# Two-operand elementwise work moved from GpSimd to VectorE in a one-core hybrid decoder step

## The chip, the cores and the metric

The kernel runs on one core of one Trainium2 chip. The metric is device time in microseconds of one execution. Five engines run their own instruction streams in order: TensorE (PE, with its weight loads as PEld), VectorE (DVE), ScalarE (ACT), GpSimd (POOL) and SyncE (SP), which issues most of the DMAs.

## The reference

One inference step of one decoder layer is computed in float32 for a prompt of 2048 tokens and for 8 sequences of 8 new tokens. With `D_MODEL = 1024`:

```
h = rmsnorm(x, norm_attn);  p = h @ w_in                      # 1024 -> 4608 columns
o_attn = sliding-window attention with sinks(p[q, k, v])
o_rwkv = rwkv7_mixer(p[rwkv part])                            # token shift, decay, matrix state, group norm
gates  = sigmoid(p[gate part] + b_gate)
merged = gates[:1024] * (o_attn @ w_branch_attn) + gates[1024:] * (o_rwkv @ w_branch_rwkv)
x = x + merged @ w_out
u = rmsnorm(x, norm_ffn) @ w_ffn_in
x = x + (gelu(causal_conv3(u[:D_FF])) * u[D_FF:]) @ w_ffn_out # D_FF = 2816
y = rmsnorm(x, norm_final)
```

The outputs are y and the new caches and states.

## The kernel before, in words

**Tiling.** The 2112 tokens are three blocks of 704, each cut in halves of 384 and 320 columns. Activations lie with features on the partitions. A weight matrix is cut in units of 128 x 1024 (512 KB): 108 for `w_in`, 24 each for the branches and for `w_out`, 132 and 66 for the two FFN matrices, over the three blocks. Each float32 value is split in a high part, rounded to the matmul type, and a low part, the difference; `mm3` (L366) multiplies high by high, high by low and low by high, so each 128-row step of a half takes three matmuls.

**A unit of weights.** `unit` loads a unit with an SP DMA, writes its high part on ACT (L347) and its low part (L353) on DVE or POOL: the counter `nw` sends every third unit to DVE, in one instruction of 1024 columns, the other two to POOL, in two instructions of 512 columns each. There are two buffers, so a unit is split while the one before it is being multiplied.

**Other two-operand work on POOL.** Part of the sums of squares for the norms (`square`, L407); the low parts of the attention queries, of half the normed inputs and of the inputs of the head sums (`split`, L358, through `halves`, `normed` and `parts`); keys times their factors in `prep` (L921, L926); the sum of the two gated branches in `branches` (L1367); and every second row of the last output (L1531 in `final_last`). POOL also does fills (memset) and two casts at the start.

**Stages.** `run` computes the inputs of the three blocks, then per block the branches, the merge and the FFN. Beside these main matmuls, which write the PSUM tiles `psd`, runs background work in generators: attention, the 64-token chunks of the RWKV recurrence, the block inverses (62 small DVE steps and two DVE transposes per half, L1088 to L1096), the `prep` of the RWKV operands, and norms.

**Order of the work.** Before each step of `mm3`, `tick` asks a planner whether a background step may go in. `account` adds the modelled cost of each instruction (`cost`) to a clock per engine, and `open` holds a step back while DVE's or ACT's clock is over 2.0 us, or POOL's over 4.0 us, ahead of PE's. `drain` runs what is left of a stream where its result is needed. Each engine runs its stream in the order in which the scheduler of the framework, which works with its own simulated times, has put it. In `account` a POOL two-operand instruction sets a window, and a DVE instruction without a PSUM operand that would start in it is put off to its end:

```
if engine == "Pool" and type(ins).__name__ == "InstTensorTensor":
    self.locked = start, start + c
elif engine == "DVE" and self.locked[0] <= start < self.locked[1] and not any(
        hasattr(a, "bass_ap") and a.bass_ap.tensor.name.startswith("ps") for a in ins.ins):
    start = self.locked[1] - 0.2
t[engine] = start + c
```

Of the kernel before, what the change touches and what calls it, by code (L numbers as in the profile page):

```python
# [100 lines left out]
class Kernel:  # L101
    def __init__(self, tc, i, o, es):
        self.tc, self.nc, self.i, self.o, self.es = tc, tc.nc, i, o, es
        pool = lambda name, bufs, **k: es.enter_context(self.pool(name, bufs, **k))
        self.cp = pool("cst", 1)
        self.dp = pool("dram", 1, space=bass.MemoryType.DRAM)
        self.sp = pool("small", 2)
        self.tp = pool("tmp", 3)
        self.wr = pool("wraw", 2)
        self.wp = pool("wsplit", 2)  # L110
        self.kp_ = pool("keep", 3)

        self.pb = {k: pool("ps" + k, n, space=bass.MemoryType.PSUM) for k, n in (("d", 3), ("r", 3), ("c", 2))}
        self.nw, self.ahead = 0, {}
# [5 lines left out]
        self.taken, self.locked = 0, (0.0, 0.0)  # L120

# [95 lines left out]
    @staticmethod  # L217
    def cost(ins, engine):
        n = 1
        for _, k in ins.outs[0].ap[1:]:  # L220
            n *= k
        if engine == "PE":
            if ins.ins[0].dtype == F32R:
                return 0.0135 + 0.000417 * n
            if ins.is_transpose:
                return 0.11 * n / 128
            if n <= 2:
                return 0.223
            return max(0.03, 0.01 + 0.00168 * n * math.prod(ins.tile_size) / (P * P))
        kind = type(ins).__name__  # L230
        if engine == "Activation":
            return 0.12 + 0.00084 * n
        two = kind == "InstTensorTensor"
        if engine == "Pool":
            return 0.1 + (0.0024 if two else 0.0009) * n
        if kind == "InstStreamTranspose":
            return 0.06 + 0.0019 * n
        full = [a for a in ins.ins if hasattr(a, "ap") and math.prod(k for _, k in a.ap[1:]) > 1]
        return 0.1 + (0.0012 if len(full) > 1 else 0.0009) * n
# [6 lines left out]
    def account(self):  # L246
# [4 lines left out]
        for k in range(self.seen, m):  # L251
# [18 lines left out]
            else:  # L270
                start = max(t[engine], t["PE"])
                if engine == "Pool" and type(ins).__name__ == "InstTensorTensor":
                    self.locked = start, start + c
                elif engine == "DVE" and self.locked[0] <= start < self.locked[1] and not any(
                        hasattr(a, "bass_ap") and a.bass_ap.tensor.name.startswith("ps") for a in ins.ins):
                    start = self.locked[1] - 0.2
                t[engine] = start + c
                self.chained = max(self.chained + c + 0.06, t[engine])
# [61 lines left out]
    def unit(self, src, w=None):  # L340
# [6 lines left out]
        nc.scalar.copy(w[:, 0], raw)  # L347
        eng = nc.gpsimd if self.nw % 3 else nc.vector
        self.nw += 1
        step = 1024 if eng is nc.vector else 512  # L350
        for u in range(0, 1024, step):
            sl = slice(u, u + step)
            eng.tensor_tensor(w[:, 1, sl], raw[:, sl], w[:, 0, sl].bitcast(F32), op=ALU.subtract)  # L353
        return w

    def split(self, hi, lo, src, eng=None):
        self.nc.scalar.copy(hi, src)  # L357
        (eng or self.nc.vector).tensor_tensor(lo, src, hi.bitcast(F32), op=ALU.subtract)  # L358

# [9 lines left out]
    def parts(self, pool, src, n, bufs=1):  # L369

        t = pool.tile([P, 2, 384], F32R, tag="parts", name="parts", bufs=bufs)
        self.split(t[:, 0, :n], t[:, 1, :n], src, self.nc.gpsimd)
        return t
# [21 lines left out]
    def squares(self, acc, x, k, n):  # L395

        nc = self.nc
        for u in range(2):
            self.square(acc[:, :n], x[:, u], k + u, n, nc.vector)

    def square(self, acc, x, k, n, eng):
        if k == 0:
# [3 lines left out]
        self.nc.scalar.activation(sq[:, :n], x, ACT.Square)  # L406
        eng.tensor_tensor(acc, acc, sq[:, :n], op=ALU.add)  # L407

# [30 lines left out]
    def normed(self, h, k, c0, n, x, pb):  # L439
# [3 lines left out]
        nc.vector.scalar_tensor_tensor(t[:, :n], x, self.par("norm_attn", k), pb[:, :n], op0=ALU.mult, op1=ALU.mult)  # L443
        self.split(h[:, k, 0, c0:c0 + n], h[:, k, 1, c0:c0 + n], t[:, :n], nc.gpsimd if k % 2 else nc.vector)

# [17 lines left out]
    def start(self, hp, xp):  # L463
# [23 lines left out]
        accs = []  # L487
        for x, (c0, n), eng in zip(xs, HALF, (nc.vector, nc.gpsimd)):
            acc = self.tp.tile([P, 384], F32, tag="acc", name="acc", bufs=2)
            accs.append(acc)  # L490
            for k in range(KT):
                self.scaled(self.h, k, c0, n, x[:, k, :n], "norm_attn")
                self.square(acc[:, :n], x[:, k, :n], k, n, eng)
        self.setup()
# [28 lines left out]
    def load_x(self, b, xp):  # L523
# [7 lines left out]
        for c0, n in HALF:  # L531
            acc = self.tp.tile([P, 384], F32, tag="acc", name="acc", bufs=2)
            for k in range(KT):
                self.square(acc[:, :n], self.xn[:, k, c0:c0 + n], k, n, nc.vector if k % 2 else nc.gpsimd)
                yield 1.0
# [112 lines left out]
    def attn_prompt(self, b, ap, t0=0, t1=T):  # L648
# [25 lines left out]
        def halves(f):  # L674
# [4 lines left out]
            k2 = ap.tile([P, 2, 256], F32R, tag="k2", name="k2")  # L679
            self.split(q2[:, 0, :, :, :nq], q2[:, 1, :, :, :nq], q[:, :, :, :nq], nc.gpsimd)  # L680
            nc.scalar.copy(k2[:, :, :nk], k[:, :, :nk])
# [202 lines left out]
    def prep(self, b, p, hf, xk, xv, xr, pp, st):  # L884
# [35 lines left out]
        nc.vector.tensor_scalar(kp[:, :n], at[:, :n], self.kah[:, p:p + 1], self.kah1[:, p:p + 1], op0=ALU.mult, op1=ALU.add)  # L920
        nc.gpsimd.tensor_tensor(kp[:, :n], kp[:, :n], xk, op=ALU.mult)  # L921
        kb = pp.tile([P, 6, 128], F32, tag="kb", name="kb")
        for sg in sgs:
            for r_ in range(2):
                rows = slice(r_ * 64, r_ * 64 + 64)
                nc.gpsimd.tensor_tensor(self.chv(kb, sg, rows, r_), self.pl(kp, sg)[rows], self.v65(ei, sg, 1)[rows], op=ALU.mult)  # L926

# [422 lines left out]
    def branches(self, b, os_, ms, gts, x):  # L1350

        nc = self.nc
        for j in range(8):
# [4 lines left out]
            for c0, n in HALF:  # L1358
                m = []
                for br in range(2):  # L1360
# [17 lines left out]
    def merge(self, b, x, ms, xp, op):  # L1378
# [14 lines left out]
        for j, hf in ((j, hf) for j in range(8) for hf in range(2)):  # L1393
# [7 lines left out]
            self.scaled(h2, j, c0, n, xv, "norm_ffn")  # L1401
            self.square(accs[hf][:, :n], xv, j, n, nc.vector if j == KT - 1 else nc.gpsimd)
            if j == KT - 1:
# [70 lines left out]
    def final(self, b, x):  # L1474
# [5 lines left out]
        def done(hf, j):  # L1480
            c0, n = HALF[hf]
            if j == 0:
                accs.append(self.tp.tile([P, 384], F32, tag="acc", name="acc", bufs=2))
            self.square(accs[hf][:, :n], x[:, j, c0:c0 + n], j, n, nc.gpsimd)
            if j == KT - 1:
# [29 lines left out]
    def final_last(self, b, x, fp):  # L1515
# [25 lines left out]
        def done(hf, j):  # L1541
            c0, n = HALF[hf]
            acc, xv = accs[hf][:, :n], x[:, j, c0:c0 + n]
            self.square(acc, xv, j, n, nc.gpsimd if j < 6 else nc.vector)
            if j == KT - 1:
# [254 lines left out]
```

## Time and profile before

| what | before |
|---|---|
| median of 3 runs (lowest to highest) | 3327.91 us (3327.47 to 3331.76) |
| the profiled execution: its time, and its span | 3327.79 us, 3326.0 us |
| mean granted TensorE clock | 0.988 |
| busy: PE, DVE, ACT, POOL | 98%, 59%, 36%, 30% |

The time of the profiled execution is 1.79 us longer than its span, from the first instruction to the last. A row of a group of instructions gives the line, the engine, the operation, the tiles written and read with their shape, the count, the busy time in us with the mean of one in ns, and the idle time of that engine just before them with what ended it. A row of the timeline gives start and duration in us of one instruction, or of a run of equal ones. A row of the waits says which engine and line waited for which, for how long in total, how often, and the longest.

### The profile page before, as it was taken

To read this page: it belongs to the slowest core of one execution; us is meant where nothing else is said; L and a number is where in the kernel's file an instruction comes from. 1 tells how busy PE (TensorE), PEld (TensorE's weight loads), DVE (VectorE), ACT (ScalarE), POOL (GpSimd) and SP (SyncE) were. 2 spreads that over 40 slices of the span, in tenths; PEclk is the share of its full clock that TensorE was granted. 3 is DMA by queue.
4 is the path that set the end of the run, shared out by engine and by line. 5 is a ranking of instruction groups with operands and counts; after the bars stand their busy time and mean duration, and the time that the engine had idled before them with its cause. 6 is when DMAs were issued, how large, how long until landed. Compare 5 with 4: busy or idle time off the path is not lost.

```text
span 3326.0 us, 60594 instructions
## 1 busy us (share of the span) xinstructions
PE 3250.5 (98%) x24072; PEld 3131.5 (94%) x24072; DVE 1948.6 (59%) x4058; ACT 1213.4 (36%) x2274; POOL 1010.1 (30%) x878
## 2 busy tenths in 40 slices
PE   8999998999999899999999999999999999999998
PEld 8998998999999789899999999999999999999998
DVE  7676568735563466577455558745456465444545
ACT  4455433333333567523232333332233233222223
POOL 3332433323223244132222254222122353222223
PEclk9999999999999899999999999999999999999999
DMA  4643443545653744233532363253313272122222
GB/s 136 182 141 117 140 152 118 146 130 159 200 171 119 221 144 118 73 80 105 153 118 87 111 225 96 82 168 110 112 65 130 70 257 70 64 70 70 70 65 75
DMA packets 335164, 408.96 MB, mean 123 GB/s; under 512 B 110496, under 2 KB 261152, under 8 KB 334624
## 3 DMA queue, kind: packets, MB, share of 16 engines
q1 hardware_dynamic: 330720, 399.31, 38.8%
q10 hardware_dynamic: 4160, 5.77, 0.5%
q8 instruction: 190, 3.11, 0.4%
q14 instruction: 94, 0.77, 0.1%
HBM read 307.55 MB, written 98.41 MB: 122 GB/s over the span
## 4 chain that ended last, share of the span: by engine, by line
PE 71%; DVE 3%; DMA 1%; issue 1%; ACT 0%; POOL 0%; SPq 0%; POOLq 0%; DVEq 0%; ACTq 0%
PE psd L366 62%; PE psr L694 1%; PE psr L743 1%; PE psc L1162 1%; PE psc L1195 1%; PE psc L1192 1%; DVE qt L1088 1%; DVE qb L1090 1%; PE psr L730 1%; DMA xd<-x 0%; PE psr L992 0%; PE psc L1019 0%; PE psc L1197 0%; PE psc L1291 0%; PE psc L1189 0%
## 5 line engine op out<-in xcount | busy, mean ns | idle before, releaser
L366 PE MATMUL psd<-o,wp 128*128 128x320 f32 (+1 forms) x8640 | 1453.6, 326 | 21.1 <-ACT o L357 10.8
L366 PEld LDWEIGHTS psd<-o,wp 128*128 128x128 f32 x8640 | 1400.9, 189 | 32.6 <-ACT o L357 11.8
L353 POOL TENSOR_TENSOR wp<-wr,wp 128x512 fp32r<-128x512 f32 x470 | 648.1, 1400 | 1675.7 <-ACT wp L347 1595.9
L366 PE MATMUL psd<-h,wp 128*128 128x320 f32 (+1 forms) x5184 | 918.1, 330 | 15.2 <-ACT wp L347 7.4
L366 PEld LDWEIGHTS psd<-h,wp 128*128 128x128 f32 x5184 | 838.4, 190 | 30.8 <-ACT wp L347 7.4
L347 ACT CAST wp<-wr 128x1024 fp32r<-128x1024 f32 x354 | 370.6, 1047 | 647.7 <-PE psd L366 587.6
L366 PE MATMUL psd<-ff,wp 128*128 128x384 f32 (+1 forms) x3168 | 526.7, 325 | 0.0
L366 PEld LDWEIGHTS psd<-ff,wp 128*128 128x128 f32 x3168 | 510.8, 188 | 3.1 <-DVE up L1434 0.2
L1470 DVE TENSOR_TENSOR x<-x,psd 128x384 f32<-128x384 f32 (+1 forms) x288 | 148.2, 519 | 236.9 <-PE psd L366 236.7
L1441 DVE TENSOR_TENSOR gb<-psd,rb 128x64 f32<-128x64 f32 (+2 forms) x154 | 70.5, 470 | 241.2 <-PE psd L366 223.7
L353 DVE TENSOR_TENSOR wp<-wr,wp 128x1024 fp32r<-128x1024 f32 x119 | 148.1, 1244 | 88.5 <-ACT wp L347 84.7
L1444 DVE SCALAR_TENSOR_TENSOR cc<-gb,pt,cc 128x704 f32<-128x704 f32 (+1 forms) x132 | 165.1, 1251 | 33.8 <-ACT cc L1442 33.0
L1442 ACT ACTIVATE cc<-gb,pt 128x64 f32<-128x64 f32 (+2 forms) x154 | 95.7, 636 | 188.6 <-DVE gb L1441 187.2
L407 POOL TENSOR_TENSOR acc<-acc,sq 128x320 f32<-128x320 f32 (+1 forms) x93 | 95.0, 1023 | 115.5 <-ACT sq L406 97.4
L1453 ACT ACTIVATE cc<-cc 128x704 f32<-128x704 f32 x66 | 52.4, 793 | 189.0 <-DVE cc L1444 119.1
L358 DVE TENSOR_TENSOR ff<-cc,ff 128x384 fp32r<-128x384 f32 (+1 forms) x132 | 92.9, 706 | 47.0 <-ACT ff L357 46.6
L1434 DVE TENSOR_TENSOR up<-psd,rb 128x384 f32<-128x384 f32 (+1 forms) x132 | 68.6, 520 | 51.7 <-PE psd L366 51.3
L357 ACT CAST ff<-cc 128x384 fp32r<-128x384 f32 (+1 forms) x132 | 63.9, 486 | 78.7 <-DVE cc L1456 78.1
L1090 DVE TENSOR_TENSOR qb<-qb,qt 128x31 f32<-128x31 f32 (+15 forms) x186 | 88.9, 478 | 4.1
L1088 DVE TENSOR_TENSOR qt<-nb,qb 128x31 f32<-128x31 f32 (+15 forms) x186 | 84.6, 455 | 3.2
L1367 POOL TENSOR_TENSOR m<-m 128x384 f32<-128x384 f32 (+1 forms) x48 | 48.8, 1018 | 118.4 <-DVE m L1364 85.2
L1456 DVE TENSOR_TENSOR cc<-cc,up 128x384 f32<-128x384 f32 (+1 forms) x132 | 71.2, 542 | 16.7 <-ACT cc L1453 13.5
(257 smaller groups left out, 3124.2 us busy)
## 6 DMA issues: line engine op xcount, KB each, us to landing
wr<-in_w_fi SPq DMA_DIRECT2D x132, 512.0 KB, 3.5
wr<-in_w_in SPq DMA_DIRECT2D x108, 512.0 KB, 4.0
wr<-in_w_fo SPq DMA_DIRECT2D x66, 512.0 KB, 3.5
cm<-md SPq DMA_DIRECT2D x33, 512.0 KB, 4.8
gt<-gd SPq DMA_DIRECT2D x48, 352.0 KB, 4.4
md<-m SPq DMA_DIRECT2D x48, 256.0 KB, 3.4
wr<-in_w_br SPq DMA_DIRECT2D x24, 512.0 KB, 4.7
wr<-in_w_out SPq DMA_DIRECT2D x24, 512.0 KB, 3.6
```

What stands on the lines that cost most here:

```text
L347: nc.scalar.copy(w[:, 0], raw)
L353: eng.tensor_tensor(w[:, 1, sl], raw[:, sl], w[:, 0, sl].bitcast(F32), op=ALU.subtract)
L358: (eng or self.nc.vector).tensor_tensor(lo, src, hi.bitcast(F32), op=ALU.subtract)
L366: nc.tensor.matmul(ps[:, :n], w[:, a, wk * 128:(wk + 1) * 128], act[:, k0 + k, b, c0:c0 + n], start=(start and k == 0 and j == 0), stop=(s ...
L407: eng.tensor_tensor(acc, acc, sq[:, :n], op=ALU.add)
L1088: nc.vector.tensor_tensor(tv, nb[:, s + 1:, s:s + 1].to_broadcast([P, k, s + 1]), qb[:, s:s + 1, :s + 1].to_broadcast([P, k, s + 1]), op=A ...
L1090: nc.vector.tensor_tensor(qb[:, s + 1:, :s + 1], qb[:, s + 1:, :s + 1], tv, op=ALU.add)
L1441: nc.vector.tensor_tensor(dst, view(ps, 0), view(rb, c0), op=ALU.mult)
L1442: nc.scalar.activation(view(c, c0), dst, ACT.Identity, bias=self.par("cb", f), scale=cw[2])
L1444: nc.vector.scalar_tensor_tensor(c[:, :npr], gb[:, u:u + npr], cw[u], c[:, :npr], op0=ALU.mult, op1=ALU.add)
L1456: nc.vector.tensor_tensor(cv, cv, up[:, c0:c0 + n], op=ALU.mult)
L1470: nc.vector.tensor_tensor(xv, xv, ps[:, :n], op=ALU.add)
```

## The change

All moved instructions go from POOL to DVE. A unit's low part is always one DVE instruction of 1024 columns; `split` and `square` lose the choice of engine. In the planner the cost of a POOL instruction becomes that of a fill, and the window that put DVE off goes. POOL keeps the fills, the two casts and the multiplications of L1531, which the diff doesn't touch.

```
-        two = kind == "InstTensorTensor"
         if engine == "Pool":
-            return 0.1 + (0.0024 if two else 0.0009) * n
+            return 0.1 + 0.0009 * n
...
-                start = max(t[engine], t["PE"])
-                if engine == "Pool" and type(ins).__name__ == "InstTensorTensor":
-                    self.locked = start, start + c
-                elif engine == "DVE" and self.locked[0] <= start < self.locked[1] and not any(
-                        hasattr(a, "bass_ap") and a.bass_ap.tensor.name.startswith("ps") for a in ins.ins):
-                    start = self.locked[1] - 0.2
-                t[engine] = start + c
+                t[engine] = max(t[engine], t["PE"]) + c
...
-        eng = nc.gpsimd if self.nw % 3 else nc.vector
-        self.nw += 1
-        step = 1024 if eng is nc.vector else 512
-        for u in range(0, 1024, step):
-            sl = slice(u, u + step)
-            eng.tensor_tensor(w[:, 1, sl], raw[:, sl], w[:, 0, sl].bitcast(F32), op=ALU.subtract)
+        nc.vector.tensor_tensor(w[:, 1], raw, w[:, 0].bitcast(F32), op=ALU.subtract)
...
-    def split(self, hi, lo, src, eng=None):
+    def split(self, hi, lo, src):
         self.nc.scalar.copy(hi, src)
-        (eng or self.nc.vector).tensor_tensor(lo, src, hi.bitcast(F32), op=ALU.subtract)
+        self.nc.vector.tensor_tensor(lo, src, hi.bitcast(F32), op=ALU.subtract)
...
-        eng.tensor_tensor(acc, acc, sq[:, :n], op=ALU.add)
+        self.nc.vector.tensor_tensor(acc, acc, sq[:, :n], op=ALU.add)
...
-        nc.gpsimd.tensor_tensor(kp[:, :n], kp[:, :n], xk, op=ALU.mult)
+        nc.vector.tensor_tensor(kp[:, :n], kp[:, :n], xk, op=ALU.mult)
...
-                nc.gpsimd.tensor_tensor(self.chv(kb, sg, rows, r_), self.pl(kp, sg)[rows], self.v65(ei, sg, 1)[rows], op=ALU.mult)
+                nc.vector.tensor_tensor(self.chv(kb, sg, rows, r_), self.pl(kp, sg)[rows], self.v65(ei, sg, 1)[rows], op=ALU.mult)
...
-                nc.gpsimd.tensor_tensor(m[0][:, :n], m[0][:, :n], m[1][:, :n], op=ALU.add)
+                nc.vector.tensor_tensor(m[0][:, :n], m[0][:, :n], m[1][:, :n], op=ALU.add)
```

The callers of `split` and `square` (`parts`, `halves`, `normed`, `start`, `load_x`, `merge`, `final`, `final_last`) drop their engine argument.

## Rows read from the trace of the kernel before

**Rows 1.** The page's first part: span, then busy time of each engine

```profile
span 3326.0 us, 60594 instructions
PE 3250.5 (98%) x24072; PEld 3131.5 (94%) x24072; DVE 1948.6 (59%) x4058; ACT 1213.4 (36%) x2274; POOL 1010.1 (30%) x878
```

**Rows 2.** The waits of PE: who waited for whom, total us, times, longest

```profile
PE psd L366 <- ACT o L357: 10.8, 2, 7.9
PE psr L1053 <- DVE nwyd L392: 8.2, 2, 5.5
PE psd L366 <- ACT wp L347: 7.4, 1, 7.4
PE psr L1053 <- DVE rbk L1031: 5.8, 1, 5.8
...
PE psd L366 <- DVE wp L353: 3.8, 2, 3.6
PE psd L366 <- DVE p L520: 3.8, 2, 2.1
PE psc L1053 <- DVE nwyd L392: 3.4, 1, 3.4
...
PE psr L980 <- DVE kb L961: 1.9, 3, 1.3
...
PE psd L366 <- POOL wp L353: 0.8, 1, 0.8
```

**Rows 3.** The chain that ended last: its longest piece, start, us, what

```profile
2813.07 491.58 PE psd L366 x3051
```

**Rows 4.** The timeline of PE at 295 us, with the wait ahead of it

```profile
294.88 5.49 PE L366 MATMUL psd<-h,wp 128*128 128x384 f32 x16 [2.06 <-DVE p L520]
```

**Rows 5.** Groups of instructions by line on POOL, over the whole span

```profile
L353 POOL TENSOR_TENSOR wp<-wr,wp 128x512 fp32r<-128x512 f32 x470 | 648.1, 1400 | 1675.7 <-ACT wp L347 1595.9 <-DVE S L1200 17.3 <-DVE o L358 15.3
L407 POOL TENSOR_TENSOR acc<-acc,sq 128x320 f32<-128x320 f32 (+1 forms) x93 | 95.0, 1023 | 115.5 <-ACT sq L406 97.4 <-DVE nwyr L387 5.0 <-ACT xs L837 4.3
L926 POOL TENSOR_TENSOR kb<-kp,ei 64x384 f32<-64x384 f32 (+3 forms) x56 | 50.5, 901 | 3.7
```

**Rows 6.** Groups of instructions by line on DVE, over the whole span

```profile
L353 DVE TENSOR_TENSOR wp<-wr,wp 128x1024 fp32r<-128x1024 f32 x119 | 148.1, 1244 | 88.5 <-ACT wp L347 84.7 <-POOL parts L358 1.5 <-issue 1.0
L1456 DVE TENSOR_TENSOR cc<-cc,up 128x384 f32<-128x384 f32 (+1 forms) x132 | 71.2, 542 | 16.7 <-ACT cc L1453 13.5
L961 DVE SCALAR_TENSOR_TENSOR kb<-at,ei 64x384 f32<-64x384 f32 (+3 forms) x56 | 34.0, 607 | 0.5
```

**Rows 7.** The timeline near the end, 3285 to 3290 us

```profile
3285.25 3.11 POOL L353 TENSOR_TENSOR wp<-wr,wp 128x512 fp32r<-128x512 f32 x2 [4.84 <-ACT wp L347]
3285.71 1.51 DVE L1444 SCALAR_TENSOR_TENSOR cc<-gb,pt,cc 128x640 f32<-128x640 f32 x1 [0.82 <-ACT cc L1442]
...
3288.37 0.87 DVE L1444 SCALAR_TENSOR_TENSOR cc<-gb,pt,cc 128x640 f32<-128x640 f32 x1
```

**Rows 8.** The timeline of DVE: first and last of 342 lengthened instructions

```profile
24.25 0.65 DVE L387 TENSOR_SCALAR nwyd<-rmsm 128x3 int32<-128x3 int32 x1
...
3308.01 0.70 DVE L390 SCALAR_TENSOR_TENSOR nwtd<-nwyd 128x3 f32<-128x3 f32 x1
```

**Rows 9.** The timeline of DVE, 561 to 570 us, before PE's wait for rbk

```profile
561.44 0.98 DVE L390 SCALAR_TENSOR_TENSOR nwtr<-nwyr 128x12 f32<-128x12 f32 x1
...
565.13 0.17 DVE L390 SCALAR_TENSOR_TENSOR nwtr<-nwyr 128x12 f32<-128x12 f32 x1
...
568.26 1.19 DVE L391 TENSOR_TENSOR nwtr<-nwtr,hsmr 128x12 f32<-128x12 f32 x1
```

**Rows 10.** The timeline of DVE, 2066 to 2071 us, before PE's wait for wp

```profile
2066.35 2.17 DVE L1094 STREAM_TRANSPOSE t<-qb 128x1024 f32<-128x1024 f32 x1
...
2068.41 1.87 DVE L1096 STREAM_TRANSPOSE qinv<-qb 128x1024 f32<-128x1024 f32 x1
```

**Rows 11.** Busy time per engine in one stretch: PE, PEld, DVE, ACT, POOL, clock

```profile
1996.00:2079.00 83.00, 79.42 (x486) 78.98 (x485) 73.84 (x129) 28.82 (x48) 38.87 (x36) 0.98 0.33 95
```

More of the change, by code (lines that the diff above doesn't have):

```diff
@@ L113, in __init__ @@
         self.pb = {k: pool("ps" + k, n, space=bass.MemoryType.PSUM) for k, n in (("d", 3), ("r", 3), ("c", 2))}
-        self.nw, self.ahead = 0, {}
+        self.ahead = {}
         self.streams = {}
@@ L119, in __init__ @@
         self.seen, self.chained, self.free = 0, 0.0, deque([0.0] * 3, 3)
-        self.taken, self.locked = 0, (0.0, 0.0)
+        self.taken = 0
     def pool(self, name, bufs=1, **k):
@@ L371, in parts @@
         t = pool.tile([P, 2, 384], F32R, tag="parts", name="parts", bufs=bufs)
-        self.split(t[:, 0, :n], t[:, 1, :n], src, self.nc.gpsimd)
+        self.split(t[:, 0, :n], t[:, 1, :n], src)
         return t
@@ L398, in squares, with square @@
         for u in range(2):
-            self.square(acc[:, :n], x[:, u], k + u, n, nc.vector)
-    def square(self, acc, x, k, n, eng):
+            self.square(acc[:, :n], x[:, u], k + u, n)
+    def square(self, acc, x, k, n):
         if k == 0:
@@ L443, in normed @@
         nc.vector.scalar_tensor_tensor(t[:, :n], x, self.par("norm_attn", k), pb[:, :n], op0=ALU.mult, op1=ALU.mult)
-        self.split(h[:, k, 0, c0:c0 + n], h[:, k, 1, c0:c0 + n], t[:, :n], nc.gpsimd if k % 2 else nc.vector)
+        self.split(h[:, k, 0, c0:c0 + n], h[:, k, 1, c0:c0 + n], t[:, :n])
     @staticmethod
@@ L487, in start @@
         accs = []
-        for x, (c0, n), eng in zip(xs, HALF, (nc.vector, nc.gpsimd)):
+        for x, (c0, n) in zip(xs, HALF):
             acc = self.tp.tile([P, 384], F32, tag="acc", name="acc", bufs=2)
@@ L492, in start @@
                 self.scaled(self.h, k, c0, n, x[:, k, :n], "norm_attn")
-                self.square(acc[:, :n], x[:, k, :n], k, n, eng)
+                self.square(acc[:, :n], x[:, k, :n], k, n)
         self.setup()
@@ L533, in load_x @@
             for k in range(KT):
-                self.square(acc[:, :n], self.xn[:, k, c0:c0 + n], k, n, nc.vector if k % 2 else nc.gpsimd)
+                self.square(acc[:, :n], self.xn[:, k, c0:c0 + n], k, n)
                 yield 1.0
@@ L679, in halves @@
             k2 = ap.tile([P, 2, 256], F32R, tag="k2", name="k2")
-            self.split(q2[:, 0, :, :, :nq], q2[:, 1, :, :, :nq], q[:, :, :, :nq], nc.gpsimd)
+            self.split(q2[:, 0, :, :, :nq], q2[:, 1, :, :, :nq], q[:, :, :, :nq])
             nc.scalar.copy(k2[:, :, :nk], k[:, :, :nk])
@@ L1401, in merge @@
             self.scaled(h2, j, c0, n, xv, "norm_ffn")
-            self.square(accs[hf][:, :n], xv, j, n, nc.vector if j == KT - 1 else nc.gpsimd)
+            self.square(accs[hf][:, :n], xv, j, n)
             if j == KT - 1:
@@ L1483, in done @@
                 accs.append(self.tp.tile([P, 384], F32, tag="acc", name="acc", bufs=2))
-            self.square(accs[hf][:, :n], x[:, j, c0:c0 + n], j, n, nc.gpsimd)
+            self.square(accs[hf][:, :n], x[:, j, c0:c0 + n], j, n)
             if j == KT - 1:
@@ L1543, in done @@
             acc, xv = accs[hf][:, :n], x[:, j, c0:c0 + n]
-            self.square(acc, xv, j, n, nc.gpsimd if j < 6 else nc.vector)
+            self.square(acc, xv, j, n)
             if j == KT - 1:
```

## The prediction

> **What bounds the kernel now.** I read the page's first part, then the waits of PE, then the chain and PE's timeline. PE is busy 3250.5 of 3326.0 us, DVE 59%, POOL 30% [rows 1]: TensorE's work is the bound and the change takes none of it away. What it can act on is the 75.5 us in which PE stands idle, and matmuls that run slowly for want of operands. Most of that idle time is visible in the waits of PE [rows 2], and the reader should sort it. The 7.4 us for the first weights and the 10.8 us at the first stage change, where inputs of the next stage come by DMA and are split on ACT, have no two-operand POOL work ahead of them. Four waits end on DVE work in the inputs of the blocks, where POOL works beside DVE: rbk 5.8, p 3.8, the norm's nwyd on psc 3.4, kb 1.9, together 14.9 us. The two waits on nwyd with psr, 8.2, are in the last 20 us. POOL itself ends only 0.8 us of PE's waiting, and low parts of weights on DVE end 3.8.
>
> Idle time isn't all. In the longest undisturbed piece 3051 matmuls take 491.58 us, 161 ns each [rows 3]. After one of the waits for p, 16 matmuls take 5.49 us instead of 2.6 [rows 4]: a stall goes on as slow matmuls that the page counts as busy, here 2.9 us behind a wait of 2.06. For the four waits I estimate 6 us of such tails, taking well under half of their 14.9 us because this row is one of the bad ones. So 20.9 us stand behind late DVE work.
>
> **What moves, in DVE time.** 470 POOL instructions on weights, 1.40 us each, become 235 on DVE; with 93 sums of squares and 56 key products that is 793.6 us of POOL's 1010.1 [rows 1, 5]. On DVE a unit's low part takes 1.244 us, an addition of 384 or 320 columns 0.542, a key product by its like 0.607 [rows 6]: 235 x 1.244 = 292, 93 x 0.542 = 50, 56 x 0.607 = 34, in all 377 us. The other 216.5 us of POOL are smaller moved groups and fills that stay; at the ratio of the sums of squares, 50 to 95, they are at most 115 us on DVE. I take 95, as most of them move: DVE gets about 470 us.
>
> **What DVE gets back.** With POOL at a low part, a DVE multiply-add of 640 columns takes 1.51 us; the same one, after POOL is done, 0.87 [rows 7]. Going through DVE's timeline, 342 single instructions that overlap a two-operand POOL instruction are over 0.1 us longer than the shortest tenth of their own shape, from the norm of the start, 0.65 us, to that of the end, 0.70 [rows 8]; summed, 264 us. This goes away with its cause. DVE then is busy for 1948.6 + 470 - 264 = 2155 us, 65% of the span. So a nearly doubled list of large work costs DVE only six points, and it is still not the bound. Two extra effects follow: small steps of a latency chain no longer wait behind POOL, and a unit's low part is done in 1.24 instead of 2.8 us once DVE gets to it.
>
> **What this is worth at PE.** The best-shown wait is rbk. Ahead of it seven small steps of the inverse root stretch over 8 us; the first took 0.98 and the last 1.19, while the same step between them, without POOL, took 0.17 [rows 9]. Over all seven the time beyond 0.17 is 5.5 us, almost the whole wait. But POOL's work of that stretch now stands in DVE's queue: two sums, one product, two key products, one low part of the head sum and one unit, 4 x 0.542 + 2 x 0.607 + 1.244 = 4.6 us [rows 6]. If all of it is queued ahead of rbk the gain is 0.9 us, if none, 5.5. I take the middle, 3.2 of 5.8, or 55%, since half of those instructions have no part in the norm and the queue is ordered by when each is ready. Applied to 20.9 us that is **-11.5**; the ends are 16% of 14.9, -2.4, and 95% of 20.9, -19.9. The 0.8 us behind POOL's low parts goes: **-0.8**.
>
> **What new waits cost.** Each unit's low part now stands in DVE's one queue. Behind it stand the DVE work of the main stage and the background, and PE needs it by the third matmul of the unit. Of the 119 units that were there before, PE waited for 3.8 us in all; at that rate 235 more cost 7.5 us. But 3.6 of the 3.8 are one wait, behind the two block transposes of an inverse, 2.17 + 1.87 us [rows 2, 10]; it is one event and no rate, and the queue in front of it was itself lengthened by POOL. I take half, **+3.7**, with 0 and 7.5 as ends. In the last 20 us ten sums of squares join DVE, 10 x 0.542 = 5.4 us, between additions that it makes at the pace of PE, while some of the small steps there get back 0.5 each [rows 8]; the last multiplications on POOL stay, and so does the wait behind them. I take **+0.5**, between -0.5 and +1.5. The branch sums, queries and normed inputs cost nothing: their consumers are a stage later, or the background, and the cover is PE's own work. If it went, each would add its own half microsecond at a stage change. Fewer POOL instructions touch no DMA: POOL issues none here, and SP's queue keeps its order.
>
> **Sum.** 3327.8 (this execution; 0.1 below the median of the runs) - 11.5 - 0.8 + 3.7 + 0.5 = 3319.7; I predict **3320**, against the median 0.24% less. A measurement of this kernel can tell about 0.2%, 6.7 us, from no change, so this is just beyond it. With all terms at their good ends it is 3306; the bad ends pass into the next case.
>
> **Rival 1: hidden anyway.** The moved work fills just the room that POOL's absence frees: 470 in, 264 out. If the queue is mostly ahead of the norm chains, the gain is -2.4 - 0.8, the new waits are +3.7 + 0.5, and the time is 3328.8. For it: PE is 98% busy, and 7.4 + 10.8 + 8.2 us of its idle time [rows 2] are not touched. Against it: the seven steps of rows 9, which were slow for no other reason. It holds from 3321.2 to 3334.5.
>
> **Rival 2, slower: late low parts.** An inverse ends with two transposes, 4.0 us that can't be split, and there are six inverses. Two in three units were on POOL and passed by them; now every unit's low part that comes due there stands behind them. Four more such waits of 3.6 us with the small gain and the tail's loss give 3327.8 + 14.4 - 3.2 + 0.5 = 3339.5. It decides from three or four hits on, where 3.6 each outweigh the 12.3 us of gain. For it: in the stretch of the merge and the inverse DVE is busy for 73.84 of 83 us before anything is added [rows 11]. Against it: POOL's 38.87 us there lengthen DVE's work too, and the scheduler knows the transposes. By the Trainium skill (Perfetto Trace Analysis, section Optimizing Scalar/DVE Operations) giving some work of a saturated VectorE to GpSimd may make sense, and taking it back, as here, would be a loss; the same section adds that the two share a port into SBUF, so that such a move might not help. The trace bears out the second half, by the pair in rows 7; the first half applies only in the stretch of rows 11, as DVE is at 59% on the whole.
>
> **Rival 3, slower: the planner holds background back.** DVE's clock now carries every unit with a room of 2.0 us, where POOL's had 4.0, so background steps may go in later, and what is left is drained at the end of the inputs, where PE has nothing else. One more loss of the size of the stage change, 10.8, gives 3338.6. Against it: the planner no longer puts DVE off for POOL, and long pieces of bare main matmuls [rows 3] show that the background is done early in the second half.
>
> **Chances.** Forecast (3306 to 3321) 0.41; rival 1 0.35; rival 2 0.16; rival 3 0.08. Hence faster 0.41, within 0.2% 0.35, slower 0.24. The range that holds 8 in 10 goes from the good end, 3306, into the slower cases up to 3338, with some tenth left out on either side; the forecast's own range is 3306 to 3321.
>
> **What would show it.** In the profile after: POOL under 60 us busy; DVE near 65%; no DVE multiply-add of 640 columns at 1.5 us; the seven steps of the norm at 0.16 to 0.2 us each and the wait for rbk under 3 us; waits of PE for low parts under 7.5 us in all. I'm wrong if PE's idle time stays at 75 us with DVE's steps short (rival 1), if waits for wp, just after transposes, pass 12 us (rival 2), or if waits gather at the drains (rival 3).

## The result and the profile after

The changed kernel takes 3303.03 us (median of 4 runs, 3299.84 to 3303.57) beside 3327.69 us for the kernel before on the same chip: a ratio of 0.9923 [0.9905, 0.994], 24.7 us or 0.77% faster. The direction was as predicted; the gain is three times the forecast's, and the time lies 3 us below the low end of the range. The profiled execution took 3303.57 us, its span is 3301.3, so the two profiled spans differ by 24.7 us as well. The intervals given for ratios reach 3 to 6 us to each side, which bears on the small differences between versions further down. Line numbers after are some 12 lower than before.

The page's first part of the kernel after:

```profile
span 3301.3 us, 60126 instructions
PE 3245.4 (98%) x24072; PEld 3129.7 (95%) x24072; DVE 2034.1 (62%) x4596; ACT 1216.4 (37%) x2276; POOL 39.6 (1%) x104
```

Beside [rows 1]: PE's idle time went from 75.5 to 55.9 us (-19.6) and its busy time fell by 5.1, with the same 24072 matmuls; together that is the 24.7. DVE has 538 instructions more and only 85.5 us more of busy time. All waits of PE in the kernel after:

```profile
PE psd L354 <- ACT o L345: 15.3, 2, 8.5
PE psd L354 <- ACT wp L340: 8.2, 1, 8.2
PE psc L1041 <- DVE nwyd L380: 4.5, 1, 4.5
PE psr L1041 <- DVE nwyd L380: 4.3, 2, 2.4
PE psd L354 <- DVE m L1352: 3.1, 2, 2.7
PE psd L354 <- DVE p L508: 2.5, 1, 2.5
PE psr L718 <- ACT ot L735: 1.7, 1, 1.7
PE psd L354 <- DVE xs L820: 1.7, 2, 0.9
PE psr L416 <- DVE acc L395: 1.6, 1, 1.6
PE psd L354 <- DVE x L1458: 0.6, 1, 0.6
PE psd L354 <- DVE gb L1429: 0.3, 1, 0.3
PE psd L354 <- DVE wp L341: 0.2, 1, 0.2
```

They sum to 44.0 us; the full list of before, of which [rows 2] shows a part, sums to 67.5. Sorted:

| waits of PE, us | before | after | change |
|---|---|---|---|
| the prediction's four: rbk, p, nwyd on psc, kb | 14.9 | 7.0 | -7.9 |
| low parts of weights, DVE and POOL | 4.6 | 0.2 | -4.4 |
| nwyd on psr | 8.2 | 4.3 | -3.9 |
| the merged inputs m | 5.6 | 3.1 | -2.5 |
| small waits of 0.2 to 2.0, 16 rows before (kt, vt, kk, grb, pT and others), five after | 16.0 | 5.9 | -10.1 |
| of these, the rows that end on DVE | 13.5 | 4.2 | -9.3 |
| ACT: the first weights, and o at the first stage change | 18.2 | 23.5 | +5.3 |

So the gain is spread over most of what waited for DVE; nwyd on psc grew, from 3.4 to 4.5 us, xs stayed at 1.7, and waits for acc and x are new. ACT's waits, which the change doesn't touch, took some back. Groups of instructions by line on DVE in the kernel after (columns as in [rows 6]):

```profile
L341 DVE TENSOR_TENSOR wp<-wr,wp 128x1024 fp32r<-128x1024 f32 x354 | 432.8, 1223 | 158.7 <-ACT wp L340 153.0 <-DMA k<-kd 0.6
L1432 DVE SCALAR_TENSOR_TENSOR cc<-gb,pt,cc 128x640 f32<-128x640 f32 x44 | 38.7, 878 | 0.0
L346 DVE TENSOR_TENSOR ff<-cc,ff 128x320 fp32r<-128x320 f32 x66 | 31.9, 484 | 0.3 <-ACT ff L345 0.3
L395 DVE TENSOR_TENSOR acc<-acc,sq 128x384 f32<-128x384 f32 x63 | 34.7, 550 | 0.7 <-ACT sq L394 0.6
```

The multiply-add of 640 columns (x44) had a mean of 1069 ns before; its mean is now 878, the undisturbed 0.87 us of [rows 7]. The `ff` low parts of 320 columns went from 843 to 484 ns. DVE's timeline after, where the norm steps of [rows 9] are:

```profile
557.00 0.17 DVE L378 SCALAR_TENSOR_TENSOR nwtr<-nwyr 128x12 f32<-128x12 f32 x1
557.21 0.17 DVE L379 TENSOR_TENSOR nwtr<-nwtr,hsmr 128x12 f32<-128x12 f32 x1
557.41 0.17 DVE L380 SCALAR_TENSOR_TENSOR nwyr<-nwtr,nwyr 128x12 f32<-128x12 f32 x1
557.62 0.56 DVE L1019 COPY rbk<-nwyr 128x768 f32<-128x768 f32 x1
```

Steps of 0.98 and 1.19 us are 0.17 now, rbk follows at once, and PE has no wait for it. Busy time per engine of the kernel after in two stretches of the first inputs (columns as in [rows 11]):

```profile
249.00:333.00 84.00, 84.00 (x571) 77.55 (x570) 56.57 (x152) 46.81 (x113) 0.21 (x2) 1.00 0.43 127
499.00:582.00 83.00, 83.00 (x610) 79.47 (x609) 60.23 (x152) 32.48 (x60) 0.57 (x4) 1.00 0.47 144
```

PE has no idle time left in either; before it was busy for 79.78 and 74.32 us of them, at a granted clock of 0.96 and 0.94 where 1.00 stands now. The first stage change, PE's timeline after:

```profile
1125.73 5.00 PE L354 MATMUL psd<-o,wp 128*128 128x384 f32 x12 [8.49 <-ACT o L345]
1137.57 7.17 PE L354 MATMUL psd<-o,wp 128*128 128x384 f32 x36 [6.84 <-ACT o L345]
```

The first matmul of the branches was at 1148.62 before, so 22.9 us are won by here; the second wait, 2.95 us before, takes 4 of them back. The chain's longest piece after:

```profile
2789.03 487.18 PE psd L354 x3021
```

It starts 24.0 us earlier than in [rows 3], at the same 161 ns per matmul. The main matmuls come in nearly the same order in both kernels; compared one by one, they are 23.7 us ahead at 731 us of the kernel before, between 14 and 33 after that, 23 to 26 from 2520 us on, and 24.7 at the last one. The gain was made in the first inputs; what came later gave some of it back and regained it.

### The profile page after: what moved, and what is told of

It reads as the page before. It is cut to its first block, busy times and chain, and to the rows that moved or that the text cites. A ratio compares the mean times of both kernels' runs of the same rounds, so it can differ in the third digit from the quotient of the medians.

```text
span 3301.3 us, 60126 instructions
## 1 busy us (share of the span) xinstructions
PE 3245.4 (98%) x24072; PEld 3129.7 (95%) x24072; DVE 2034.1 (62%) x4596; ACT 1216.4 (37%) x2276; POOL 39.6 (1%) x104
## 4 chain that ended last, share of the span: by engine, by line
PE 97%; DMA 1%; DVE 1%; ACT 0%; issue 0%; POOL 0%; SPq 0%; POOLq 0%; ACTq 0%; DVEq 0%
PE psd L354 83%; PE psr L980 1%; PE psr L682 1%; PE psr L731 1%; PE psr L718 1%; PE psc L1150 1%; PE psc L1180 1%; PE psc L1183 1%; PE psr L870 1%; PE psc L1007 0%; DMA xd<-x 0%; PE psc L1185 0%; PE psc L1177 0%; PE psr L968 0%; PE psr L1007 0%; PE psc L1279 0%
## 5 line engine op out<-in xcount | busy, mean ns | idle before, releaser
L354 PE MATMUL psd<-o,wp 128*128 128x320 f32 (+1 forms) x8640 | 1451.1, 326 | 18.8 <-ACT o L345 15.3
L341 DVE TENSOR_TENSOR wp<-wr,wp 128x1024 fp32r<-128x1024 f32 x354 | 432.8, 1223 | 158.7 <-ACT wp L340 153.0
L1432 DVE SCALAR_TENSOR_TENSOR cc<-gb,pt,cc 128x704 f32<-128x704 f32 (+1 forms) x132 | 121.9, 924 | 2.4 <-ACT cc L1430 1.7
L346 DVE TENSOR_TENSOR ff<-cc,ff 128x384 fp32r<-128x384 f32 (+1 forms) x132 | 68.5, 520 | 30.8 <-ACT ff L345 30.5
L1297 ACT ACTIVATE g<-psd,der 128x384 f32<-128x384 f32 (+1 forms) x64 | 35.4, 553 | 136.5 <-PE psd L354 88.7
L624 ACT ACTIVATE s<-s,nm 128x256 f32<-128x256 f32 (+2 forms) x136 | 65.7, 485 | 29.8 <-DVE nm L619 27.1
L1352 DVE SCALAR_TENSOR_TENSOR m<-gt,psd 128x384 f32<-128x384 f32 (+1 forms) x96 | 49.6, 518 | 39.4 <-PE psd L354 38.6
L825 ACT ACTIVATE xs<-psd,der 128x384 f32<-128x384 f32 (+1 forms) x56 | 31.1, 555 | 107.4 <-PE psd L354 107.4
L395 DVE TENSOR_TENSOR acc<-acc,sq 128x384 f32<-128x384 f32 (+1 forms) x126 | 65.3, 518 | 6.3 <-ACT sq L394 5.6
```

The lines of the kernel that those rows point to most:

```text
L341: nc.vector.tensor_tensor(w[:, 1], raw, w[:, 0].bitcast(F32), op=ALU.subtract)
L346: self.nc.vector.tensor_tensor(lo, src, hi.bitcast(F32), op=ALU.subtract)
L354: nc.tensor.matmul(ps[:, :n], w[:, a, wk * 128:(wk + 1) * 128], act[:, k0 + k, b, c0:c0 + n], start=(start and k == 0 and j == 0), stop=(s ...
L395: self.nc.vector.tensor_tensor(acc, acc, sq[:, :n], op=ALU.add)
L624: nc.scalar.activation(s[:nq, h, :nk], s[:nq, h, :nk], ACT.Exp, bias=nm[:nq, h:h + 1], scale=0.125, accum_out=rs[:nq, h:h + 1])
L1432: nc.vector.scalar_tensor_tensor(c[:, :npr], gb[:, u:u + npr], cw[u], c[:, :npr], op0=ALU.mult, op1=ALU.add)
```

## Experiments

The theory, A below, is that POOL's two-operand work lengthens DVE's, which is late for PE. Its rivals: the planner's window was what cost time (B); low parts come earlier, whoever blocks whom (C); DVE time costs PE nothing as long as PE doesn't wait for it.

**Parts of the change.** `units_only`: before, with only the weights' low parts on DVE.

```
-        eng = nc.gpsimd if self.nw % 3 else nc.vector
...
-            eng.tensor_tensor(w[:, 1, sl], raw[:, sl], w[:, 0, sl].bitcast(F32), op=ALU.subtract)
+        nc.vector.tensor_tensor(w[:, 1], raw, w[:, 0].bitcast(F32), op=ALU.subtract)
```

> The kernel before with only the low parts of the weights all on DVE; the rest stays on POOL, and so does the planner with its window. Before is 3327.7 us, after 3303.0, a gain of 24.7. Theory A (port): what costs time is DVE standing still while POOL reads SBUF for a two-operand instruction; the low parts are 648 of the 974 us of that, so two thirds of the gain: 3311. Theory B (planner): the gain comes from the planner without its window, which sends background steps elsewhere; the window is still set here by the remaining POOL work, so at most a third: 3320 or more. Theory C (low parts sooner): PE gets a unit's low part after 1.2 instead of 2.8 us; all of the gain: 3303.

`rest_only`: after, with two of three units' low parts back on POOL and the planner of before.

```
-        nc.vector.tensor_tensor(w[:, 1], raw, w[:, 0].bitcast(F32), op=ALU.subtract)
+        eng = nc.gpsimd if self.nw % 3 else nc.vector
...
+            eng.tensor_tensor(w[:, 1, sl], raw[:, sl], w[:, 0, sl].bitcast(F32), op=ALU.subtract)
```

> The kernel after with two in three units' low parts on POOL again, with the planner of before. Theory A: a third of the gain, 326 of 974 us of POOL's reading are gone: 3319. Theory B: the window is set by the units as before: 3325 to 3328. Theory C: nothing, 3327.

`window_off`: before, without the planner's window.

```
-                elif engine == "DVE" and self.locked[0] <= start < self.locked[1] and not any(
-                        hasattr(a, "bass_ap") and a.bass_ap.tensor.name.startswith("ps") for a in ins.ins):
-                    start = self.locked[1] - 0.2
```

> The kernel before with the planner's window alone taken out: all work stays where it is, only DVE is no longer put off in the planner's clock. If the planner's clock was part of the gain of the change: 3310 to 3322. If only the chip's blocking counts: the same as before within 4 us, 3323 to 3331, or slower, since the clock now knows less of what happens.

| run | median us | ratio to before [95%] |
|---|---|---|
| units_only | 3294.64 | 0.9905 [0.9891, 0.9918] |
| rest_only | 3313.68 | 0.9964 [0.9952, 0.9977] |
| window_off | 3329.92 | 1.0009 [1.0, 1.0017] |

The window isn't it: without it the kernel is no faster, and `units_only`, which keeps it, gains. Earliness alone isn't it either: `rest_only` leaves two thirds of the low parts on POOL and gains 13.5 us, where C allowed none. But A's own times, 3311 and 3319, were missed too, by 16 and 5 us on the fast side: the gain doesn't go by the share of POOL's time. Either half of the moves gains, the units 32.5 us and the rest 13.5, but together they gain 24.7: after the units, moving the rest costs 8.4. The waits of PE in `units_only`, the longest:

```profile
PE psd L361 <- ACT wp L347: 8.2, 1, 8.2
PE psd L361 <- ACT o L352: 8.2, 2, 7.6
PE psc L1048 <- DVE nwyd L387: 4.4, 1, 4.4
```

The wait for `o` is 8.2, not 15.3. SP's queue shows a difference at this place. In the kernel after:

```profile
1121.77 1.80 SPq L1304 DMA_DIRECT2D ol<-od  x4
1123.69 2.06 SPq L1364 DMA_DIRECT2D x<-in_xT  x4
1126.69 0.34 SPq L1304 DMA_DIRECT2D ol<-rd  x1
```

Four loads of x, 2.9 MB in all, that the merge needs only later stand ahead of the last loads of `ol`, from which `o` is made. In `units_only` x is issued at 1132.29, behind them, and PE's second wait is 0.64 instead of 6.84. My prediction's "SP's queue keeps its order" held for the source only; the scheduler set another order.

**The stage change.** So x's loads were put two units later, in four versions: after, `units_only`, before and `rest_only`.

```
-            if j == 2:
+            if j == 4:
                 self.load_x1(b, x)
```

> The kernel after with the four loads of x for the merge issued at the fifth unit of the branches instead of the third. In the kernel after PE stands 6.84 us at the first stage change for two halves of o whose loads (ol<-rd) SP issued behind 2.9 MB of x; with only the low parts moved they went ahead of x and the wait was 0.64. If that order is what makes the change as made slower than its larger half: 3295 to 3298. If the sums, splits and products on DVE are what costs, 3301 to 3304.

> The kernel with only the low parts moved, and the loads of x later as well. There the loads of o already go ahead of x at the first stage change, so by the theory of SP's order it gains at most 2 us: 3292 to 3295. It is the candidate to beat both kernels.

> The kernel before with the loads of x at the fifth unit of the branches. With units_x_late (3288.9), rest_x_late and x_late (3291.6) it makes a square in which the place of those loads is the same. In the kernel before SP issues the loads of o's second half ahead of x, and PE's wait there is 2.95 us: it gains at most 3 us by the theory of SP's order, 3323 to 3327. If later loads of x help every version alike by the 11.4 us that they gave the kernel after: 3315.

> The kernel with all but two thirds of the low parts on DVE, and x later. PE's waits at the first stage change are 3.9 us in the version without it, so 3310 to 3314. If the other work is worth something by itself once SP's order is out of the way, it stays 10 or more below before_x_late; if it only pays for itself, within 5 of it.

| low parts on DVE | rest on DVE | median us | x later: run, median us | ratio to before [95%] |
|---|---|---|---|---|
| no | no | 3327.1 | before_x_late, 3319.34 | 0.9977 [0.9968, 0.9986] |
| no | yes | 3313.68 | rest_x_late, 3301.55 | 0.9925 [0.9911, 0.9939] |
| yes | no | 3294.64 | units_x_late, 3288.91 | 0.9886 [0.9873, 0.99] |
| yes | yes | 3303.03 | x_late, 3291.60 | 0.9893 [0.988, 0.9907] |

In `x_late` the wait for `o` is 9.7 and the second gap 0.57. But x later helps all four versions, by 6 to 12 us, where by SP's order I had expected at most 3 for before and 2 for `units_only`, and 3310 to 3314 us for `rest_x_late`: a gain of its own, independent of the change. In before and `rest_only` it shows in PE's waits for m, which fall from 5.6 to 0.7 and from 9.0 to 1.0 us. With it the units are worth 30.4, the rest alone 17.8, both 27.7. Of the 8.4 us that the rest seemed to cost on top of the units, 5.7 belonged to this order; 2.7 remain, less than the runs of the two versions differ among themselves (3286.8 to 3292.8 and 3289.2 to 3294.3). `units_x_late` has the lowest median of all, 1.14% below before.

**Reading or occupying.** Three kernels put a load back beside the changed kernel, at those units that POOL used to split. `reads_beside`: two idle POOL instructions that read and write SBUF.

```
         nc.vector.tensor_tensor(w[:, 1], raw, w[:, 0].bitcast(F32), op=ALU.subtract)
+        if self.nw % 3:
+            for u in (0, 512):
+                self.idle.add(nc.gpsimd.tensor_tensor(raw[:, u:u + 512], w[:, 0, u:u + 512].bitcast(F32),
+                                                      w[:, 0, u:u + 512].bitcast(F32), op=ALU.mult).ins.name)
+        self.nw += 1
```

> The kernel after with 470 idle POOL multiplications of 128x512 that read the high part of a unit twice and write into the raw weights' buffer once that is free; no one reads what they write and the planner does not count them. Theory A: POOL's reading blocks DVE as before, while DVE also has the moved work: at least two thirds of the gain is lost, 3319 to 3330. Theories B and C: nothing is lost, 3303 to 3306.

`fills_beside`: as much POOL time in fills, which only write.

```
+            for u in range(5):
+                self.idle.add(nc.gpsimd.memset(raw[:, :512], 0.0).ins.name)
```

> The same with five POOL fills of 128x512 in place of two multiplications, which write the same buffer and read nothing; POOL is busy about as long. Theory A: fills do not hold up DVE's instructions with two SBUF operands, 3303 to 3306. If POOL's work itself, or the raw buffer held longer, were what costs, it would be the same as with the multiplications. Theories B and C: 3303 to 3306.

`low_twice`: a second subtraction on DVE at the same units, into the raw buffer.

```
+            nc.vector.tensor_tensor(raw, raw, w[:, 0].bitcast(F32), op=ALU.subtract)
```

> The kernel after with a second subtraction on DVE, of the same shape and length, for two in three units (236 x 1.22 = 288 us more on DVE, into the raw buffer, counted by the planner). If a low part that joins DVE's queue costs PE what the prediction's rate says, 0.032 us each, it is 3303 + 7.5 = 3310 or more. If DVE has room for it in the order that the scheduler makes, 3303 to 3306.

The same three with x later, and the last one with the second subtraction left off the planner's clock:

> reads_beside with the loads of x at the fifth unit, so that the traffic at the stage change is out of the way; beside fills_beside_x and x_late (3291.6). Blocking as the cause: 20 or more above fills_beside_x, as it was 21.7 without. If a good part of that difference was the stage change: under 12.

> fills_beside with x later. The 7.8 us that the fills cost came with waits at the stage change of 18.4 against 15.3 us, from the raw buffer held longer beside x: if that is all, 3291 to 3295. If fills block DVE after all, 3298 or more.

> low_twice (3339.6, 36.5 above the kernel after) with x later. PE never waited for a low part there; its waits for o at stage changes were 29.9 us against 15.3, as the background was not done. If the extra load acts through the stage changes: at least 15 of the 36 stay, 3306 or more. If most of it was the traffic there: 3292 to 3300.

> The same second subtractions, with x later, but not on the planner's clock: DVE has the load, and background steps are placed as without it. If the planner's holding back of background is what the load costs: within 8 of x_late, up to 3300. If DVE itself is late with it, PE waits for steps of the background: as low_twice_x or worse.

| added to the kernel after | median us (over after) | with x later (over x_late) |
|---|---|---|
| POOL reads | 3332.53 (+29.5) | 3313.31 (+21.7) |
| POOL fills | 3310.84 (+7.8) | 3299.09 (+7.5) |
| second DVE subtraction | 3339.56 (+36.5) | 3324.88 (+33.3) |
| the same, not counted by the planner | | 3319.85 (+28.3) |

The ratios to before are 1.0015 [1.0006, 1.0024], 0.9952 [0.994, 0.9964] and 1.0035 [1.0022, 1.0047]; with x later 0.9966 [0.9954, 0.9978], 0.992 [0.9907, 0.9934], 0.9996 [0.9987, 1.0005] and 0.9981 [0.9972, 0.999]. The page's first part of `reads_beside`:

```profile
PE 3256.2 (98%) x24072; PEld 3137.8 (94%) x24072; DVE 2188.7 (66%) x4596; ACT 1213.5 (36%) x2276; POOL 609.1 (18%) x576
```

The same of `fills_beside`:

```profile
PE 3245.4 (98%) x24072; PEld 3129.8 (95%) x24072; DVE 2043.9 (62%) x4596; ACT 1217.1 (37%) x2276; POOL 663.4 (20%) x1284
```

The multiply-add's group on DVE, in `reads_beside`:

```profile
L1439 DVE SCALAR_TENSOR_TENSOR cc<-gb,pt,cc 128x640 f32<-128x640 f32 x44 | 48.2, 1095 | 0.0
```

And in `fills_beside`:

```profile
L1438 DVE SCALAR_TENSOR_TENSOR cc<-gb,pt,cc 128x640 f32<-128x640 f32 x44 | 38.7, 879 | 0.0
```

With more POOL time than the reads, the fills leave the multiply-add at 879 ns; the reads bring it to 1095 and DVE to 155 us more. It is the reading that lengthens DVE's two-operand work. The Trainium skill (SBUF — State Buffer, section Who interferes with whom) says just this: a DVE instruction with two SBUF inputs contends with a GpSimd instruction that reads SBUF, not with one that only writes it. The two rows agree. The difference in time between the two kernels, 21.7 us, is the price of reading instead of filling; with x later it is 14.2, between the 20 that I had named for blocking and the 12 for the stage change.

That fills cost 7 us at all was not expected (3303 to 3306; 3295 at most with x later). By what I had written, 3298 or more with x later would mean that fills block DVE, and in part they do. Copies with one operand in SBUF are lengthened by fills; this is the copy of two columns per tile, after and in `fills_beside`:

```profile
L1407 DVE COPY gb<-chalo 128x2 f32<-128x2 f32 x66 | 10.6, 160 | 0.4
L1413 DVE COPY gb<-chalo 128x2 f32<-128x2 f32 x66 | 18.0, 272 | 0.4
```

Copies and operations with a scalar (TENSOR_SCALAR) take 19.5 us longer in `fills_beside` than after, those with two operands the same time. `o` is waited for 18.4 us there beside 15.3 after. The fills hold the raw buffer on average 3.0 us beyond the low part, the reads 2.5 and the second subtraction 1.9, so the longer hold can hardly account for more than the fills' 7 to 8 us in any of the three.

The doubled subtraction refutes the last rival. PE waits for low parts for 0.3 us in all in `low_twice`, yet it loses 36.5 us. Its longest wait:

```profile
PE psd L357 <- ACT o L348: 29.9, 4, 16.0
```

DVE is busy 2276.6 us there, 242.5 more than after, so one microsecond of added DVE time cost about 0.15. It comes out where the background must be finished, at the second stage change. Up to there the main matmuls run ahead of those of the kernel after, by 31 us at 1811 us, since the planner holds background back; behind it they are 26 late. Busy time per engine in that stretch (columns as in [rows 11]), after and in `low_twice`:

```profile
1860.00:1990.00 130.00, 127.29 (x787) 126.96 (x786) 84.60 (x161) 38.23 (x59) 3.34 (x5) 0.99 0.51 169
1860.00:1990.00 130.00, 107.30 (x749) 100.24 (x746) 86.00 (x179) 41.46 (x79) 0.31 (x1) 0.87 0.50 163
```

Leaving the second subtraction off the planner's clock gives back only 5.0 us, which is hardly clear of noise, but the loss moves: `low_uncounted_x` is 11 us behind `x_late` already in the inputs, at 378 us, and has no jump at the second stage change. So DVE's load costs about as much either way, as background held back or as work that is late.

**Where the reads cost.** `reads_beside`, at units below 108 (72 units, the inputs) or from 108 on (164 units) alone.

```
-        if self.nw % 3:
+        if self.nw < 108 and self.nw % 3:
```

> As reads_beside (3332.5 against fills 3310.8), but the idle reading multiplications only at the first 108 units, the inputs, where short DVE steps stand in chains that PE waits for: 72 of 236 units, 31% of the reads. By share of reads: a loss of 9 against the kernel after. If the chains of the inputs are where blocking costs: a loss of 15 to 25, 3318 to 3328.

> The same at the other 164 units, 69% of the reads, beside branches, merges and FFN. By share of reads: a loss of 20, 3323. If blocking costs little where PE has long runs of main matmuls: a loss of 3 to 12, 3306 to 3315.

They take 3314.35 and 3314.28 us, 0.9962 [0.9949, 0.9974] and 0.9964 [0.9952, 0.9977]: +11.3 each over after, 0.157 us per unit in the inputs and 0.069 later. The inputs, full of latency chains, are 2.3 times as sensitive, but I had expected 15 to 25 us there; the later stages, with 3 to 12 expected, are not free. The two losses add up to 22.6 us, all reads together cost 29.5.

**Blocking or earliness.** If POOL's low parts become fills of like duration, they are as late as before but read nothing; with short fills they are early too; the low part of these units stays zero. Here `low_fills_long` has four and three fills, `low_fills_short` one and one.

```
+        if eng is nc.gpsimd:
+            for u, times in ((0, 4), (512, 3)):
+                for _ in range(times):
+                    nc.gpsimd.memset(w[:, 1, u:u + 512].bitcast(F32), 0.0)
```

> The kernel before, in which POOL writes zeros as the low parts of two units in three, by seven fills of 128x512 (3.9 us, about as long as ACT's rounding and POOL's subtractions took after the buffer was free); this leaves out that part of the weights' precision. POOL no longer reads SBUF there, DVE gets no more work, and the low parts are there as late as before. If blocking is what two thirds of the gain were: at or below units_only, 3285 to 3297. If it was that low parts came sooner: 3323 to 3328.

> The same with two fills, 1.1 us, so that low parts are there sooner too. What it gains over low_fills_long is what earlier low parts are worth: within 3 us by the theory of blocking, most of the gain by the other.

They take 3307.72 us, 0.9942 [0.9929, 0.9956], and 3299.01 us, 0.9919 [0.9905, 0.9932]. The page's first part of `low_fills_long`:

```profile
PE 3254.0 (98%) x24072; PEld 3136.1 (95%) x24072; DVE 1775.5 (54%) x4058; ACT 1215.9 (37%) x2276; POOL 1148.1 (35%) x2058
```

DVE runs the same 4058 instructions as in [rows 1] in 173.1 us less, although POOL is busy for 138 us more, and the time is 18.0 us less. POOL's low parts are done 2.4 us after the high part on average, 3.0 in the kernel before, so little of this is earliness. It isn't the whole of the blocking, as the fills bring a blocking of their own. A DVE copy and POOL's seven fills in `low_fills_long`:

```profile
1669.12 3.66 DVE L1454 COPY chalo<-gb 128x2 f32<-128x2 f32 x1
1669.43 3.32 POOL L353 MEMSET wp<- 128x512 f32 x7
```

The copy ends with the fills. These 44 copies have a mean of 919 ns there, 385 in `low_fills_short` and 194 before. I had expected 3297 at most. `low_fills_short` gains a further 8.7, from low parts that are there as soon as the high part and from fewer fills; the two weren't separated. So of this 26.7 at least two thirds is the end of POOL's reading, and at most a third the earliness, within the noise of the runs (3302.4 to 3313.9 for the long fills). The split is approximate: each edit gets a new order from the scheduler.

## Why the prediction was right in direction and too small

**What moves, right.** The 538 instructions that joined DVE take 453 us there by their groups; I had 470. POOL is at 39.6 us, under 60.

**What DVE gets back, too small.** DVE is busy for 2034.1 us, not 2155. The groups of DVE instructions whose shape and count are the same in both kernels lose 317 us, not 264. My count took only rows of single instructions; the same rule over all DVE instructions, runs of equal ones included, finds 423 of them and 327 us, and those under 0.1 us would add only 4. The sum also set durations against busy time: 453 - 317 is 136, but busy time grew by only 85.5, since successive instructions overlap by 42 us more than before and a few in groups of changed count got shorter as well.

**The blocked chains, right for what it counted.** Of the four waits' 14.9 us, 7.9 went, 53% where I took 55%. The tails were put at 6 us, 55% of which is 3.3; PE's busy time fell by 5.1. Together that is -13.0 against the -11.5 of this term, but the 5.1 is of the whole kernel, so that the match is partly luck. rbk's wait went wholly, the best case of that row's two ends. Reads put beside the changed kernel bring the four to 11.7 us, fills to 7.2.

What a tail is, I had wrong. The 16 slow matmuls of [rows 4] were not short of operands. Busy time per engine in that stretch before, with the granted clock third from the end:

```profile
294.88:300.40 5.52, 5.52 (x17) 5.30 (x17) 1.86 (x6) 1.72 (x3) 0.00 (x0) 0.50 0.65 182
```

PE had stood still for 0.41, 0.56 and 2.06 us just before; TensorE then ran at the lower of its two clocks, 1.2 instead of 2.4 GHz, at 343 ns per matmul where [rows 3] has 161 at full clock. So the clock belongs in the price of a wait.

**The failed step is the first: "Four waits end on DVE work in the inputs of the blocks".** It limited the gain to four rows of the list. The cause that I gave for them, DVE steps lengthened by POOL's reads, acts on any wait for DVE. The small rows that end on DVE, 13.5 us, fell to 4.2, with no term in the sum. Other runs bear out the cause: such rows sum to 12.4 us with reads put back beside the changed kernel, 5.4 with fills, and 1.9 in `low_fills_long`, where nothing moved to DVE. I had the evidence in hand, 342 lengthened instructions from the start to the end [rows 8], and applied it to the largest rows of one stage. The fall of m by 2.5, also without a term, is not of this kind: with x later, m is 0.7 in the kernel before and 1.0 after.

**The second failed step is the new waits, wrong sign.** I took +3.7 for 235 low parts in DVE's one queue. The waits for low parts fell from 4.6 to 0.2, POOL's -0.8 among them: 7.3 us off. The two transposes of an inverse still take 4.2 us, but a low part now takes 1.22 and the unit before it is out ahead of them. DVE's timeline after:

```profile
2050.18 1.22 DVE L341 TENSOR_TENSOR wp<-wr,wp 128x1024 fp32r<-128x1024 f32 x1
...
2053.02 2.23 DVE L1082 STREAM_TRANSPOSE t<-qb 128x1024 f32<-128x1024 f32 x1
2055.14 2.00 DVE L1084 STREAM_TRANSPOSE qinv<-qb 128x1024 f32<-128x1024 f32 x1
...
2059.83 1.23 DVE L341 TENSOR_TENSOR wp<-wr,wp 128x1024 fp32r<-128x1024 f32 x1 [1.10 <-ACT wp L340]
```

DVE idles for 1.10 us before the next low part, waiting for ACT: the transposes were done in time. That the one wait of 3.6 went doesn't need the move: in `rest_only`, with two thirds of the low parts on POOL, PE waits for low parts for 0.3 us in all. Which part of the change ended it stays open.

**The tail, about right.** Predicted +0.5, measured 0.0: from the end of the last main matmul to the end of the span it is 18.05 us before and 18.06 after. PE's waits there fell from 8.2 to 3.5 us, but the stretch behind PE's last matmul grew from 7.5 to 11.5, as POOL now makes its last multiplications for both halves in one go. That they would stay and decide was foreseen. The rest of the 4.3 us on nwyd with psr is a new wait of 2.4 behind the first stage change.

**Not foreseen: +5.3 at ACT's waits**, which the prediction called untouched. Most of it is the order of loads at the first stage change, and `units_only` and `x_late` show it as such.

Added up: -7.9 for the four waits, -4.4, -3.9, -2.5, -10.1 and +5.3 make -23.5 in the list of waits; idle time that the list doesn't show grew by 3.9, that behind PE's last matmul, and PE's busy time fell by 5.1. That is -24.7, 16.6 more than the forecast's -8.1. The small rows on DVE (9.3) and the waits for low parts (7.3) make up as much; the rest cancels.

**The rivals.** Rival 1 (hidden anyway) falls: PE's idle time didn't stay. Rival 2 falls with the 0.2 us for low parts, and by `units_only`, the cleanest form of what it feared, which gained 32.5 us. The Trainium skill (Perfetto Trace Analysis, section Optimizing Scalar/DVE Operations) says that offloading to GpSimd may make sense when VectorE is saturated, and warns of the port that the two share. VectorE is at 59% to 62% here, so no run tests the first half; the runs with reads bear out the second, by 21.7 us. Rival 3 didn't decide, but its mechanism exists: in `low_twice` background is held back and time is lost at the second stage change.

**Open.** Why x's later loads help every version was not shown. How the fills' 7 to 8 us divide between longer copies and the raw buffer held longer was not tried. That both halves together gain less than the units alone is partly the order of loads (5.7 of 8.4); the remaining 2.7 may be DVE's added load, the scheduler's order or noise.

## What to carry to other kernels

When one engine's reads slow another engine's instructions everywhere, price the change on every wait that ends on the slowed engine, small rows included, not only on the largest ones of one stage. An engine at 60% is not free: here each added microsecond on DVE cost 0.12 to 0.15 at the end with hardly a visible wait for the added work. So try the hot part alone (here the weights' low parts): it was as fast as moving all, or faster. After any edit look again at the DMA order at stage changes; here later loads of x moved the time by up to half of what the change itself gave.

## What the runs showed of the hardware that was not expected

- GpSimd fills of 663 us beside DVE left its two-operand work at its own pace (879 ns against 878), while 609 us of reads put 217 ns on each 640-column multiply-add.
- Fills do block DVE's copies: one of two columns took 3.66 us beside seven fills, and 0.15 to 0.17 wherever no POOL instruction ran beside it.
- The contention reaches the smallest steps: DVE instructions of 12 columns took 0.98 and 1.19 us under POOL's reads, and 0.17 without.
- After a wait of 2.06 us the granted TensorE clock stood at 0.50, and matmuls took 343 ns instead of 161.
- 2.9 MB of loads issued two units later were worth 6 to 12 us in four versions of the kernel.
